# Residual parked in the output rows, twenty tiles for the squares, three sweeps

## The chip, the cores and the metric

One core of one Trainium2 chip runs the whole program. The metric is device time in microseconds; for the kernel before it is the median of three runs. A profiled execution gives the trace.

## What is computed

One layer of a hybrid encoder trunk: 256 tokens, width 2048, hidden width 8192, all in float32. The second half of it, the MLP, is where the change lies:

```python
u = _rms_norm(x, norm_mix_pre[l])
mix = hybrid_mixer(u, ...)                     # three branches, gated, @ w_out
x = x + _rms_norm(mix, norm_mix_post[l])       # the residual, called x1 in the kernel
hdn = jnp.square(jax.nn.relu(_rms_norm(x, norm_mlp_pre[l]) @ w_mlp_up[l]))
x = x + _rms_norm(hdn @ w_mlp_down[l], norm_mlp_post[l])
```

The residual is needed three times: transposed, as the input of the MLP; squared and summed, for the small term that stands for epsilon in the last norm; and at the very end, where the normed MLP output is added to it.

## The kernel before

**Arithmetic.** Every float32 weight is cast to a high part on ScalarE (`whi`, L173) and the rest is kept as a low part by a subtraction on VectorE (`wlo`, L175). A product of two split operands is three TensorE products: high by high, high by low, low by high. All weights come as blocks of 128 x 1024, 512 KB, through SP's queue into a few rotating `raw` buffers (three in L161, six of `raw2` in L1326). `pk` is a pool of 24 tiles of 128 x 512.

**The mixer** ends in `tok` (L208), four column groups of 512 for two token halves. `rstd_of` (L1139) forms a reciprocal root: a sum on VectorE, ScalarE adds the last part, GpSimd raises to -0.5 (L1148). `add_mixed` (L1166) then adds the normed mixer output to `x1`, two tiles of 128 x 2048, in pieces of 512 columns. In this part the order of TensorE, ScalarE, VectorE and GpSimd is the order in which the program is written, up to L1275. TensorE transposes `x1` (`turn`, L1188), `cut` scales and splits it into the sixteen `pk` tiles `upk2`, and the first up products start.

**Up.** For each of 64 hidden blocks of 128, `up(j)` is two halves of 16 matmuls (eight of 512 columns, eight of 256). `hidden(j)` adds two parts of the result, takes the positive part, squares it and keeps it in a `pk` tile, two blocks to a tile.

**Down.** Fourteen sets (`SIZES`) of four hidden blocks go through a scheme of the Strassen and Winograd kind: instead of eight block products, seven (`F[1]` to `F[7]`, six matmuls of 128 x 512 each), at the price of sums. `forms(m)` makes seven combinations of the squares for two hidden blocks, high and low, in two tiles of the tag `fm`; the pool has 16 of them, the room for eight pairs, four sets. Sums of weights are made by `prep` (L1404): one or two additions of 128 x 1024 on VectorE (L1407) and additions by DMA from GpSimd (L1410). The last two sets' worth (eight blocks) goes through a plain `tok` at the end, the tail.

The sets are grouped into sweeps: (3, 4, 4, 3). Within a sweep the seven PSUM sums run over its sets, for one half of the output columns, then for the other. At the end of each such round the seven sums are added into `ys` (`post`, L1446, the operations of L1437): eleven additions on VectorE and one copy on ScalarE; in the first sweep four of the eleven are copies on ScalarE (L1442). Eight rounds make eight of these ends.

**The order of the work.** A list is built (L1520 to L1556) and driven by `drive`. It begins with up halves and six forms, then has 28 slots, one for each set and column half. A slot holds the seven products, three or four up halves (three in the slots named in `THREE`) and those forms for which there is room and whose squares exist. In a slot with four halves products and halves alternate; in one with three, products 4, 7, 1 and 6 follow each other. The additions of a finished round are handed out two with each up half. From L1275 on the scheduler of the framework puts the engines' instructions in order from this list; it may move them where an operand is ready sooner.

**The squares of the residual.** `hidden` for j from 2 to 9 also issues one ScalarE square of 512 columns of `x1` with a running sum (L1357), eight in all, each behind the square of its block; j = 10 and 11 make the two small columns `eps4` on VectorE.

**The end.** In the tail, for each of four column groups and two token halves: add the sum to `ys`, square it, scale by the gain; the gains come as four loads of 256 KB into `pk` tiles, called one by one from `side` at each new weight block. For the last group the reciprocal root is formed and five operations (L1584) add the scaled output to `x1` and five DMAs write the rows.

Of the kernel before, what the change touches and what calls it, by code (L numbers as in the profile page):

```python
# [11 lines left out]
F32 = mybir.dt.float32  # L12
F32R = mybir.dt.float32r
AF = mybir.ActivationFunctionType
ALU = mybir.AluOpType
AX = mybir.AxisListType
# [3 lines left out]
D = 2048  # L20
# [4 lines left out]
EPS = 1e-6  # L25
# [27 lines left out]
def hybrid_block(ctx, tc, xt, x, gains, params, consts, lora, gup, wst, out):  # L53
    nc = tc.nc
    V, A, G, PE = nc.vector, nc.scalar, nc.gpsimd, nc.tensor

    cpool = ctx.enter_context(tc.tile_pool(name="cpool", bufs=1))
# [8 lines left out]
    def nm(s):  # L66
        uid[0] += 1
        return f"{s}_{uid[0]}"
# [7 lines left out]
    def pk():  # L76
        return pkpool.tile([128, 512], F32R, tag="pk", name=nm("pk"), bufs=24)

    def tmp(n=T):
        return tpool.tile([128, T], F32, tag="tmp", name=nm("tmp"), bufs=3)  # L80
# [75 lines left out]
    side = []  # L156
# [125 lines left out]
    def g1(w=T):  # L282
        return rp.tile([128, T], F32, tag="g1", name=nm("g1"), bufs=21)
# [83 lines left out]
    w = {(u, 0): [wpool.tile([128, HALF], F32R, tag=t, name=nm(t), bufs=3) for t in ("whi", "wlo")] for u in range(3)}  # L367
# [662 lines left out]
    for br in ("sb", "fox"):  # L1030
        for s in ("q", "k"):
# [3 lines left out]
            for h in range(4):  # L1035
                ps = unit(upk)
                t = g1()
# [91 lines left out]
    p2 = ctx.enter_context(tc.tile_pool(name="p2", bufs=1))  # L1129
    po = ExitStack()  # L1130
    op = po.enter_context(tc.tile_pool(name="op", bufs=1))

    def gain(n, tiles):

        t = [a if a.dtype == F32 else a.bitcast(F32) for a in tiles]
        return t, [lambda g=g: nc.sync.dma_start(out=t[g], in_=gains[n:n + 1, 512 * g:512 * g + 512]
                                                 .to_broadcast([128, 512])) for g in range(4)]

    def rstd_of(ss, eps, sums):  # L1139

        if sums is None:
            sums = cpool.tile([128, 1], F32, name=nm("ssum"))
            V.tensor_reduce(sums, ss[:, 0:3], AX.X, ALU.add)
            V.tensor_scalar(sums, sums, 1.0 / D, eps, ALU.mult, ALU.add)
            return sums
        r = cpool.tile([128, 1], F32, name=nm("rs"))
        A.activation(r, ss[:, 3:4], AF.Identity, scale=1.0 / D, bias=sums)
        G.tensor_tensor(r, r, cst[:, 2:3], ALU.pow)  # L1148
        return r
# [2 lines left out]
    for f in now:  # L1152
        f()
    loads = []
    x1 = [p2.tile([128, D], F32, tag="x1", name=nm("x1"), bufs=2) for _ in range(2)]
    for c in range(0, D, 512):
        for tt in range(2):
            loads.append(lambda tt=tt, c=c: nc.sync.dma_start(out=x1[tt][:, c:c + 512],
                                                              in_=x[tt * 128:tt * 128 + 128, c:c + 512]))
# [3 lines left out]
    def junk():  # L1163
        return p2.tile([128, 512], F32, tag="junk", name=nm("junk"), bufs=2)

    def add_mixed(tt, c, w):  # L1166
        V.scalar_tensor_tensor(x1[tt][:, c:c + w], mg[tt][:, c:c + w], r2[tt], x1[tt][:, c:c + w], ALU.mult, ALU.add)

# [88 lines left out]
    for b in range(4):  # L1259
        add_mixed(1, 512 * b, 512)  # L1260
        turn(1, b)
# [14 lines left out]
    ss3 = cpool.tile([128, 2, 4], F32, name="ss3")  # L1276
# [11 lines left out]

    SIZES = (3, 4, 4, 3)
    THREE = (18, 20, 21, 23, 24, 25, 26, 27)
    LAST = sum(SIZES)
    AF_ = {1: 0, 2: 1, 4: 2, 7: 3, 5: 4, 6: 5, 3: 6}
    work, posts, sums, hl = [], [], [], {}
# [41 lines left out]
    eps4, sum4 = [], []  # L1337
    ss4 = cpool.tile([128, 2, 4], F32, name="ss4")
    ys = []
    hid, fmh, fml = {}, {}, {}  # L1340

    squares = [(tt, c) for c in range(4) for tt in range(2)]

    def hidden(j, ps):

        b, t = tmp(), tmp()
        A.activation(b, ps[:, T:2 * T], AF.Copy)  # L1347
        V.tensor_tensor(t, ps[:, 0:T], b, ALU.add)
        A.activation(t, t, AF.Relu)
        if j % 2 == 0:  # L1350
            hid[j // 2] = pk().bitcast(F32).rearrange("p (s t) -> p s t", s=4)
        h = hid[j // 2]
        last = A.activation(h[:, 0:4:3] if j % 2 == 0 else h[:, 1:3], t.rearrange("p (s t) -> p s t", s=2), AF.Square)
        if j >= 2 and squares:
            tt, c = squares.pop(0)
            with tc.issue_after(last.ins):
                A.activation(junk(), x1[tt][:, 512 * c:512 * c + 512], AF.Square, accum_out=ss3[:, tt, c:c + 1])  # L1357
        if j in (10, 11):
            e = cpool.tile([128, 2], F32, name=nm("eps4"))
            V.tensor_reduce(e[:, 0:1], ss3[:, j % 2, :], AX.X, ALU.add)  # L1360
            V.tensor_scalar(e[:, 0:1], e[:, 0:1], 1.0 / D, EPS, ALU.mult, ALU.add)
            V.tensor_tensor(e[:, 1:2], e[:, 0:1], e[:, 0:1], ALU.mult)
            V.tensor_scalar(e[:, 1:2], e[:, 1:2], EPS, None, ALU.mult)
            eps4.append(e[:, 1:2])

    def up(j):

        ps = [None]

        def run(hl, half):  # L1370
            if half == 0:
                ps[0] = gps()
            gemm(ps[0], hl[0], hl[1], upk2[8 * half:8 * half + 8], half == 0, half == 1)
            if half:
                posts.append(lambda: hidden(j, ps[0]))

        n = base + 64 * (j // KT) + 2 * (j % KT)
        return [(lambda half=half: wq.pop(0) if wq else parts(wraw(n + half)), lambda hl, half=half: run(hl, half), 2)
                for half in range(2)]
# [15 lines left out]
    def down(q, sb):  # L1395

        d0 = sum(SIZES[:q])
        dn = d0 + SIZES[q] - 1
        Q, R, vx = {}, {}, {}
# [74 lines left out]
    p3 = ctx.enter_context(tc.tile_pool(name="p3", bufs=1))  # L1474

    def fm():
        return p3.tile([128, 7, 128], F32R, tag="fm", name=nm("fm"), bufs=16)

    def split3(m):

        h = hid.pop(m)
        for i in range(2):
            t = fm().rearrange("p a b -> p (a b)")[:, 0:512]
            src = h[:, 0:4:3] if i == 0 else h[:, 1:3]
            hi = t[:, 0:T].rearrange("p (s t) -> p s t", s=2)
            A.activation(hi, src, AF.Copy)
            V.tensor_tensor(t[:, T:].rearrange("p (s t) -> p s t", s=2), src, hi.bitcast(F32), ALU.subtract)
            hp[2 * m + i] = t
# [14 lines left out]
    for j in range(2):  # L1503
        hidden(j, gp[j])
    ups = [it for j in range(2, 64) for it in up(j)]
    made, room = [0], [8]

    def some(n):

        return [ups.pop(0) for _ in range(min(n, len(ups)))]  # L1510

    def form(need=32):

        if room[0] == 0 or 128 - len(ups) < 4 * (made[0] + 1) or made[0] >= need:
            return []
        room[0] -= 1
        made[0] += 1
        return [later(made[0] - 1)]

    work.extend(form())  # L1520
    while made[0] < 2 * SIZES[0]:
        work.extend(some(4) + form())
    drive()
    ys.extend(p2.tile([128, D], F32, tag="y", name=nm("y"), bufs=2) for _ in range(2))
# [3 lines left out]
    NUM = [4] * 28  # L1528
    for g in THREE:
        NUM[g] = 3  # L1530
    assert sum(NUM) == left
    last, count, free = [], 0, 0
    first = [sum(SIZES[:q]) for q in range(len(SIZES) + 1)]

    needs = [2 * (first[q] + d + 1) if sb == 0 else 2 * first[q + 1]
             for q in range(len(SIZES)) for sb in range(2) for d in range(SIZES[q])] + [32] * 3
    for q in range(len(SIZES)):
        for sb in range(2):
            for d, F in enumerate(down(q, sb)):
# [10 lines left out]
                last, count, free = [F[4]], count + 1, sb  # L1550
# [8 lines left out]
    hp = [hp[k] for k in range(4 * LAST, 64)]  # L1559
    g4, loads = gain(1, [pk() for _ in range(4)])  # L1560
    side.extend(loads)

    def spare(n):

        if n < wst.shape[0] - 3:
            return None
        return [p3.tile([128, HALF], F32, tag="raw2", name=nm("kw"), bufs=6).bitcast(F32R) for _ in range(2)]

    home[0] = spare
    for g in range(4):  # L1570
        gs = slice(512 * g, 512 * g + 512)
        for tt, ps in enumerate(tok(hp, 4 if g == 3 else 1)):
            yv = ys[tt][:, gs]
            V.tensor_tensor(yv, yv, ps, ALU.add)
            A.activation(junk(), yv, AF.Square, accum_out=ss4[:, tt, g:g + 1])
            if g == 3:
                r4 = rstd_of(ss4[:, tt, :], None, sum4[tt])
            V.tensor_tensor(yv, yv, g4[g], ALU.mult)
            if g == 2:
                sum4.append(rstd_of(ss4[:, tt, :], eps4[tt], None))  # L1580
            if g == 3:
                for c, w in (0, 512), (512, 512), (1024, 512), (1536, 256), (1792, 256):
                    cs = slice(c, c + w)
                    V.scalar_tensor_tensor(x1[tt][:, cs], ys[tt][:, cs], r4, x1[tt][:, cs], ALU.mult, ALU.add)  # L1584
                    (nc.scalar if c == 512 or w == 256 and c == 1536 else nc.sync).dma_start(
                        out=out[tt * 128:tt * 128 + 128, cs], in_=x1[tt][:, cs])


# [123 lines left out]
```

## Time and profile before

| what | value |
|---|---|
| median of three runs | 1504.24 us (1503.12 to 1506.56) |
| profiled execution | 1505.64 us, of which the span is 1503.8 us |
| granted TensorE clock | 0.998 |
| TensorE busy | 1489.7 us, 8384 matmuls |
| VectorE busy | 1206.8 us |
| ScalarE busy | 938.4 us |
| GpSimd busy | 91.1 us |
| bytes moved by DMA | 312.19 MB, read from HBM 279.24 MB, written 2.10 MB |

The profile's page gives busy times per engine, the span in forty slices, the chain of work that ended last, groups of instructions with their mean duration, and DMA issues with the time to landing. The trace behind it answers for a stretch of time: which instructions ran, what each waited for, and how busy each engine was. In a row of the timeline stand the start, the duration, the engine and line, the operation, the tiles (written <- read) and in brackets the idle time before it and what ended that. PE is TensorE, PEld its weight loads, DVE VectorE, ACT ScalarE, POOL GpSimd, SP the queue that issues most DMAs.

The span falls into the mixer (to about 820 us), the opening of the MLP with up halves alone (to 888 us), the 28 slots (to 1450 us), the tail of plain products (to 1494 us) and the last writes.

### The profile page before, as it was taken

The numbers are of one execution on the slowest core, as the hardware profiler recorded it, in microseconds if no ns is written. First come the engines' busy times: TensorE is split into PE (matmuls) and PEld (weight loads), VectorE is DVE, ScalarE is ACT, GpSimd is POOL, SyncE is SP. The second block draws the span as 40 slices with busy tenths as digits, with TensorE's granted clock in tenths as the row PEclk, the third lists the DMA queues.
The fourth block names the chain that finished last, engine by engine and source line by source line (L and its number), as shares of the span: only waits on it lengthen the run. The fifth ranks groups of instructions, "written<-read, shape, count | busy, mean of one in ns | idle before, by whom it ended". The sixth has DMA issues, their size and how long they took to land.

```text
span 1503.8 us, 22719 instructions
## 1 busy us (share of the span) xinstructions
PE 1489.7 (99%) x8384; PEld 1250.7 (83%) x8384; DVE 1206.8 (80%) x1677; ACT 938.4 (62%) x1435; POOL 91.1 (6%) x151
## 2 busy tenths in 40 slices
PE   9999999999999999999999999999999999999997
PEld 7888888887788887788888888888888888888886
DVE  7965679895688796476657788999899989999996
ACT  7665677545776445564445776776767666767663
POOL 0011003000001000000000000000000000000000
PEclk9999999999999999999999999999999999999999
DMA  8545445454445455345674768879888888889874
GB/s 284 202 150 178 151 158 169 155 182 162 157 167 173 150 192 189 135 165 195 226 243 161 261 179 256 252 223 286 243 269 239 225 279 258 249 259 261 256 216 149
DMA packets 107055, 312.19 MB, mean 208 GB/s; under 512 B 12352, under 2 KB 14400, under 8 KB 106944
## 3 DMA queue, kind: packets, MB, share of 16 engines
q1 hardware_dynamic: 96336, 279.35, 54.8%
q0 software_dynamic: 8064, 29.36, 10.5%
q10 hardware_dynamic: 2544, 2.03, 0.5%
q8 instruction: 66, 1.08, 0.3%
q14 instruction: 45, 0.37, 0.1%
HBM read 279.24 MB, written 2.10 MB: 187 GB/s over the span
## 4 chain that ended last, share of the span: by engine, by line
PE 94%; DVE 2%; ACT 1%; issue 1%; DMA 0%; SPq 0%; POOLq 0%; DVEq 0%; POOL 0%; ACTq 0%
PE gps L235 27%; PE gps L191 22%; PE gps L195 12%; PE gps L220 7%; PE mps L1430 3%; PE mps L1432 3%; PE mps L1431 3%; PE gps L1432 2%; PE gps L1430 2%; PE gps L1431 2%; PE gps L197 2%; DVE wlo L175 1%; PE mps L836 1%; PE gps L359 1%; PE gps L1219 1%
## 5 line engine op out<-in xcount | busy, mean ns | idle before, releaser
L175 DVE TENSOR_TENSOR wlo<-raw,whi 128x1024 fp32r<-128x1024 f32 x570 | 691.3, 1223 | 151.5 <-ACT whi L173 141.8
L173 ACT ACTIVATE whi<-raw 128x1024 fp32r<-128x1024 f32 x570 | 597.9, 1057 | 246.5 <-PE gps L235 71.7
L191 PE MATMUL gps<-pk,whi 128*128 128x512 f32 x1460 | 370.7, 392 | 1.0 <-ACT whi L173 0.8
L191 PEld LDWEIGHTS gps<-pk,whi 128*128 128x128 f32 x1460 | 270.6, 188 | 56.4 <-ACT whi L173 1.7
L235 PE MATMUL gps<-whi,pk 128*128 128x512 f32 x1004 | 253.5, 392 | 0.0
L195 PEld LDWEIGHTS gps<-pk,wlo 128*128 128x128 f32 x1561 | 212.8, 190 | 15.4 <-DVE wlo L175 0.5
L235 PEld LDWEIGHTS gps<-whi,pk 128*128 128x128 f32 x1004 | 186.4, 188 | 40.0 <-issue 1.0
L195 PE MATMUL gps<-pk,wlo 128*128 128x256 f32 x1561 | 218.0, 282 | 0.1
L235 PE MATMUL gps<-wlo,pk 128*128 128x512 f32 x502 | 138.1, 393 | 0.1
L235 PEld LDWEIGHTS gps<-wlo,pk 128*128 128x128 f32 x502 | 93.1, 188 | 20.0 <-DVE wlo L175 0.5
L1347 ACT ACTIVATE tmp<-gps 128x256 f32<-128x256 f32 x64 | 24.6, 385 | 105.2 <-PE gps L197 103.3
L1430 PE MATMUL mps<-whi,fm 128*128 128x512 f32 x224 | 88.6, 396 | 1.4 <-ACT whi L173 1.3
L1431 PE MATMUL mps<-whi,fm 128*128 128x512 f32 x224 | 87.7, 392 | 0.0
L1432 PE MATMUL mps<-wlo,fm 128*128 128x512 f32 x224 | 87.4, 390 | 0.0
L1410 POOL DMA_DIRECT2D raw<-raw x56 | 48.8, 872 | 571.9 <-DVE raw L1407 279.8
L1407 DVE TENSOR_TENSOR raw<-raw,raw 128x1024 f32<-128x1024 f32 x56 | 68.4, 1222 | 0.8
L1430 PE MATMUL gps<-whi,fm 128*128 128x512 f32 x168 | 65.8, 392 | 0.0
L1432 PE MATMUL gps<-wlo,fm 128*128 128x512 f32 x168 | 65.7, 391 | 0.0
L1431 PE MATMUL gps<-whi,fm 128*128 128x512 f32 x168 | 65.5, 390 | 0.0
L220 PE MATMUL gps<-whi,pk 128*128 128x512 f32 x224 | 60.8, 393 | 0.0
L1430 PEld LDWEIGHTS mps<-whi,fm 128*128 128x128 f32 x224 | 42.3, 189 | 9.7 <-ACT whi L173 3.5
L1432 PEld LDWEIGHTS mps<-wlo,fm 128*128 128x128 f32 x224 | 42.1, 188 | 9.4
(358 smaller groups left out, 1743.0 us busy)
## 6 DMA issues: line engine op xcount, KB each, us to landing
raw<-in_wst_dram SPq DMA_DIRECT2D x510, 512.0 KB, 4.3
raw<-raw POOLq DMA_DIRECT2D x56, 512.0 KB, 7.2
x<-in_xt_dram SPq DMA_DIRECT2D x8, 256.0 KB, 5.6
x<-in_x_dram SPq DMA_DIRECT2D x8, 256.0 KB, 5.5
raw<-in_wst_dram SPq DMA_DIRECT2D x6, 256.0 KB, 4.9
pk<-in_wst_dram SPq DMA_DIRECT2D x6, 256.0 KB, 5.1
g<-in_gains_dram SPq DMA_DIRECT2D x4, 256.0 KB, 5.0
pk<-in_gains_dram SPq DMA_DIRECT2D x4, 256.0 KB, 6.8
```

What stands on the lines that cost most here:

```text
L173: A.activation(hi, raw, AF.Copy)
L175: low = lambda: V.tensor_tensor(lo, raw, hi.bitcast(F32), ALU.subtract)
L191: PE.matmul(ps, hi[:, i * 128:i * 128 + 128], pks[i], start=first and i == 0, stop=False)
L195: PE.matmul(ps[:, 0:T], lo[:, i * 128:i * 128 + 128], pks[i][:, 0:T], start=False, stop=False)
L197: PE.matmul(ps, hi[:, (n - 1) * 128:n * 128], pks[n - 1], start=False, stop=True)
L220: PE.matmul(ps[tt], pks[k][:, c:c + 128], w[:, (k - k0) * 512:(k - k0) * 512 + 512], start=k == 0 and part == 0 and w is hl[0], stop=w is ...
L235: PE.matmul(ps[tt], pks[k][:, c:c + 128], w[:, (k - k0) * 512:(k - k0) * 512 + 512], start=k == 0 and part == 0 and w is hl[0], stop=False)
L1407: V.tensor_tensor(R[d, a], R[d, a], R[d, b], ALU.add)
L1410: G.dma_start(out=R[d, a], in_=R[d, b], accum_op=ALU.add)
L1430: PE.matmul(Q[f], a, w, start=d == d0 and i == 0, stop=False)
L1431: PE.matmul(Q[f], b, w, start=False, stop=False)
L1432: PE.matmul(Q[f], a, wl, start=False, stop=d == dn and i == 1)
```

## The change

`x1` moves from the pool that lives to the end (`p2`) to one that is closed before the squares' room is opened (`op`). Each piece that `add_mixed` finishes is written to its place in the output by a DMA on GpSimd's queue, eight of 256 KB. The freed 16 KB of each partition give four more tiles of the tag `fm`: 20, the room for five sets. The sweeps become (5, 5, 4), six rounds instead of eight; `THREE` has twelve slots instead of eight; one more form and four more up halves stand ahead of the first slot. The squares of the residual leave `hidden`. At the end the residual is read back into eight `pk` tiles by SP's queue, two at once and six from `side` behind the gains; a new function `moment` squares it in the second column group of the tail and makes `eps4`; the last additions use these tiles and write from them.

```diff
-    x1 = [p2.tile([128, D], F32, tag="x1", name=nm("x1"), bufs=2) for _ in range(2)]
+    x1 = [op.tile([128, D], F32, tag="x1", name=nm("x1"), bufs=2) for _ in range(2)]
...
         V.scalar_tensor_tensor(x1[tt][:, c:c + w], mg[tt][:, c:c + w], r2[tt], x1[tt][:, c:c + w], ALU.mult, ALU.add)
+        G.dma_start(out=out[128 * tt:128 * tt + 128, c:c + w], in_=x1[tt][:, c:c + w])
...
-    SIZES = (3, 4, 4, 3)
-    THREE = (18, 20, 21, 23, 24, 25, 26, 27)
+    SIZES = (5, 5, 4)
+    THREE = (13, 17, 18, 20, 21, 9, 22, 23, 24, 25, 26, 27)
...
-        last = A.activation(h[:, 0:4:3] if j % 2 == 0 else h[:, 1:3], t.rearrange("p (s t) -> p s t", s=2), AF.Square)
-        if j >= 2 and squares:
-            tt, c = squares.pop(0)
-            with tc.issue_after(last.ins):
-                A.activation(junk(), x1[tt][:, 512 * c:512 * c + 512], AF.Square, accum_out=ss3[:, tt, c:c + 1])
-        if j in (10, 11):
-            e = cpool.tile([128, 2], F32, name=nm("eps4"))
...
+        A.activation(h[:, 0:4:3] if j % 2 == 0 else h[:, 1:3], t.rearrange("p (s t) -> p s t", s=2), AF.Square)
+
+    def moment(tt):
+
+        for c in range(4):
+            A.activation(junk(), x1b[tt, c], AF.Square, accum_out=ss3[:, tt, c:c + 1])
+        e = cpool.tile([128, 2], F32, name=nm("eps4"))
...
-        return p3.tile([128, 7, 128], F32R, tag="fm", name=nm("fm"), bufs=16)
+        return p3.tile([128, 7, 128], F32R, tag="fm", name=nm("fm"), bufs=20)
...
-    made, room = [0], [8]
+    made, room = [0], [10]
...
-    while made[0] < 2 * SIZES[0]:
+    while made[0] < 7:
         work.extend(some(4) + form())
...
+    def back(tt, c):
+        x1b[tt, c] = pk().bitcast(F32)
+        nc.sync.dma_start(out=x1b[tt, c], in_=out[128 * tt:128 * tt + 128, 512 * c:512 * c + 512])
+
+    for tt in range(2):
+        back(tt, 0)
+        side.append(lambda tt=tt: [back(tt, c) for c in range(1, 4)])
...
+            if g == 1:
+                moment(tt)
...
-                    V.scalar_tensor_tensor(x1[tt][:, cs], ys[tt][:, cs], r4, x1[tt][:, cs], ALU.mult, ALU.add)
+                    o = x1b[tt, c // 512][:, c % 512:c % 512 + w]
+                    V.scalar_tensor_tensor(o, ys[tt][:, cs], r4, o, ALU.mult, ALU.add)
                     (nc.scalar if c == 512 or w == 256 and c == 1536 else nc.sync).dma_start(
-                        out=out[tt * 128:tt * 128 + 128, cs], in_=x1[tt][:, cs])
+                        out=out[tt * 128:tt * 128 + 128, cs], in_=o)
```

More of the change, by code (lines that the diff above doesn't have):

```diff
@@ L1340, in hybrid_block @@
     hid, fmh, fml = {}, {}, {}
-    squares = [(tt, c) for c in range(4) for tt in range(2)]
     def hidden(j, ps):
@@ L1352, in hidden @@
         h = hid[j // 2]
-        last = A.activation(h[:, 0:4:3] if j % 2 == 0 else h[:, 1:3], t.rearrange("p (s t) -> p s t", s=2), AF.Square)
-        if j >= 2 and squares:
-            tt, c = squares.pop(0)
-            with tc.issue_after(last.ins):
-                A.activation(junk(), x1[tt][:, 512 * c:512 * c + 512], AF.Square, accum_out=ss3[:, tt, c:c + 1])
-        if j in (10, 11):
-            e = cpool.tile([128, 2], F32, name=nm("eps4"))
[L1360 to L1364, printed above, removed]
+        A.activation(h[:, 0:4:3] if j % 2 == 0 else h[:, 1:3], t.rearrange("p (s t) -> p s t", s=2), AF.Square)
[3 more added lines that the diff above has]
+        e = cpool.tile([128, 2], F32, name=nm("eps4"))
+        V.tensor_reduce(e[:, 0:1], ss3[:, tt, :], AX.X, ALU.add)
+        V.tensor_scalar(e[:, 0:1], e[:, 0:1], 1.0 / D, EPS, ALU.mult, ALU.add)
+        V.tensor_tensor(e[:, 1:2], e[:, 0:1], e[:, 0:1], ALU.mult)
+        V.tensor_scalar(e[:, 1:2], e[:, 1:2], EPS, None, ALU.mult)
+        eps4.append(e[:, 1:2])
     def up(j):
@@ L1561, in hybrid_block @@
     side.extend(loads)
+    x1b = {}
+    def back(tt, c):
[4 more added lines that the diff above has]
+        side.append(lambda tt=tt: [back(tt, c) for c in range(1, 4)])
     def spare(n):
```

## The prediction

> **What bounds the kernel now.** I read the page's busy totals first, then the chain that ended last, then the groups.
>
> ```profile
> PE 1489.7 (99%) x8384; PEld 1250.7 (83%) x8384; DVE 1206.8 (80%) x1677; ACT 938.4 (62%) x1435; POOL 91.1 (6%) x151
> PE 94%; DVE 2%; ACT 1%; issue 1%; DMA 0%; SPq 0%; POOLq 0%; DVEq 0%; POOL 0%; ACTq 0%
> L1437 DVE TENSOR_TENSOR y<-y,mps 128x512 f32<-128x512 f32 x30 | 20.1, 682 | 0.0
> L1437 DVE TENSOR_TENSOR y<-y,junk 128x512 f32<-128x512 f32 x22 | 15.1, 686 | 0.1
> L1437 DVE TENSOR_TENSOR junk<-junk,gps 128x512 f32<-128x512 f32 x16 | 10.9, 681 | 0.0
> L1437 DVE TENSOR_TENSOR y<-y,gps 128x512 f32<-128x512 f32 x12 | 8.2, 680 | 0.0
> ```
>
> TensorE is the bound: 94% of the chain is PE. The change adds and removes no matmul, so it can win only what PE loses by waiting in the stretch where products and up halves are interleaved. Its length follows from PE's timeline and two links of the chain.
>
> ```profile
> 882.72 2.00 PE L191 MATMUL gps<-pk,whi 128*128 128x512 f32 x8
> 885.51 1.78 PE L191 MATMUL gps<-pk,whi 128*128 128x512 f32 x7
> 888.31 0.40 PE L1430 MATMUL gps<-whi,fm 128*128 128x512 f32 x1
> 901.06 1.81 PE gps L191 x8
> 921.76 1.81 PE gps L191 x8
> 1450.37 1.98 PE L235 MATMUL gps<-whi,fm 128*128 128x512 f32 x8
> ```
>
> An up half costs 885.51 - 882.72 = 2.79 us; a slot with four halves recurs after 921.76 - 901.06 = 20.70, so one with three takes 17.91. The 28 slots (20 and 8) need 557.3 us; first product to tail they took 1450.37 - 888.31 = 562.06. **So 4.8 us is the ceiling of the gain there.** The timeline shows where it went: beside 0.1 at 894.6, seven places in which a matmul starts over 0.33 us after the one before, where 0.23 is usual. First and last:
>
> ```profile
> 1196.89 1.06 ACT L173 ACTIVATE whi<-raw 128x1024 fp32r<-128x1024 f32 x1 [3.21 <-DMA raw<-in_wst_dram]
> 1198.69 0.39 PE L1432 MATMUL gps<-wlo,fm 128*128 128x512 f32 x1
> 1199.74 0.50 PE L1430 MATMUL mps<-whi,fm 128*128 128x512 f32 x1 [0.66 <-ACT whi L173]
> 1414.01 0.39 PE L1432 MATMUL gps<-wlo,fm 128*128 128x512 f32 x1
> 1414.44 0.50 PE L1430 MATMUL mps<-whi,fm 128*128 128x512 f32 x1
> ```
>
> Summed over 0.23 a step they lose 1.46 (at 1198.7), 0.83 (1269.1), 0.31 (1319.7), 0.31 (1354.5), 0.89 (1364.9), 0.28 (1401.7), 0.31 (1414.0): 4.4. By slot, counted from 0, that is slots 14-15, 18, 21, 22, 23, 25, 26: all but one in or next to slots with three halves. The busy times in stretches of one slot (us, then PE, PEld, DVE, ACT, POOL, clock, DMA share, GB/s; slots 8, 9, 10, 13, 14, 20, 22, 23, 24, 25) show VectorE nearly as full as PE:
>
> ```profile
> 1054.09:1074.81 20.72, 20.72 (x108) 17.74 (x107) 18.05 (x20) 13.96 (x21) 1.74 (x2) 1.00 0.87 260
> 1074.81:1095.53 20.72, 20.72 (x108) 17.74 (x107) 20.04 (x24) 13.62 (x20) 1.74 (x2) 1.00 0.80 235
> 1095.53:1116.25 20.72, 20.72 (x108) 17.74 (x107) 18.86 (x21) 13.22 (x19) 1.74 (x2) 1.00 0.89 270
> 1157.70:1178.42 20.72, 20.72 (x107) 17.73 (x107) 20.51 (x25) 14.55 (x21) 1.74 (x2) 1.00 0.83 243
> 1178.42:1199.14 20.72, 20.66 (x106) 17.34 (x104) 19.35 (x26) 13.42 (x19) 1.74 (x2) 1.00 0.83 228
> 1299.96:1317.89 17.93, 17.93 (x94) 15.33 (x93) 17.11 (x20) 12.97 (x17) 1.74 (x2) 1.00 0.84 237
> 1335.81:1356.54 20.73, 20.69 (x106) 17.39 (x105) 20.50 (x26) 13.95 (x19) 1.74 (x2) 1.00 0.81 237
> 1356.54:1374.47 17.93, 17.31 (x88) 14.44 (x87) 16.22 (x19) 12.55 (x17) 1.74 (x2) 1.00 0.98 278
> 1374.47:1392.39 17.92, 17.92 (x92) 15.20 (x91) 17.23 (x20) 12.41 (x19) 1.74 (x2) 1.00 0.90 254
> 1392.39:1410.32 17.93, 17.92 (x91) 14.88 (x90) 17.65 (x20) 11.93 (x16) 1.74 (x2) 1.00 0.90 257
> 1268.29 1.28 DVE L1437 TENSOR_TENSOR y<-y,mps 128x512 f32<-128x512 f32 x2
> ```
>
> **The change, part by part: the sweeps.** A round (one sweep, one column half) ends in 11 adds on VectorE, 7 in the first sweep. Eight rounds make 80, which are the four L1437 groups; six make 14 + 44 = 58. Off VectorE go 22 x 0.68 = 15.0 us. An add inside a run costs 0.64 (the pair in 1.28). From slots 9 and 10 (11 adds, no form) a four-half slot needs (20.04 + 18.86 - 7.04) / 2 = 15.9 of VectorE; a form is slot 8 less that, 2.1; slots 24 and 25 (11 adds) give a three-half slot 13.9. By the lists, forms and adds fall so that slots 6, 14 and 22 need over 105% of their PE time (22.7, 23.3, 23.9 of 20.7): they lost 0, 1.46 and 1.20 (slot 22's 0.31 and the 0.89 right behind it), 0.89 in the mean. Of the other three-half slots, 18, 21, 24, 25, 27, with adds, lost 0.83, 0.31, 0, 0.28, 0: mean 0.28; 20 and 26, without, 0 and 0.31: 0.15.
>
> After the change only slot 20 is over 105%: 13.9 + 5 adds + 1 form = 19.2 of 17.9. But three-half slots grow from 8 to 12 (9, 13, 17, 18, 20 to 27), since four more up halves and one form move ahead of the first slot; there VectorE has room, and the 4 x 2.79 us of PE only change place. With adds are 9, 23, 24, 27 (4 x 0.28 = 1.1), without 13, 17, 18, 21, 22, 25, 26 (7 x 0.15 = 1.1), and slot 20 loses 0.9; 0.1 elsewhere. Sum 3.2 against 4.5 (the seven places and 0.1): **-1.3 us**. Bounds: -4.8 if all loss goes; above, every one of the last eight slots loses slot 23's 0.89 (rival B).
>
> **Residual written out.** Eight more POOL issues follow the residual adds, four before the second reciprocal root in POOL's program order, so that one queues behind them, and VectorE's second residual adds, PE's transposes and the MLP's start behind it.
>
> ```profile
> 811.61 2.73 DVE L1167 SCALAR_TENSOR_TENSOR x<-mg,rs,x 128x512 f32<-128x512 f32 x4
> 819.02 0.56 POOL L1148 TENSOR_TENSOR rs<-rs,cst 128x1 f32<-128x1 f32 x1 [8.91 <-ACT rs L1147]
> 821.27 2.73 DVE L1167 SCALAR_TENSOR_TENSOR x<-mg,rs,x 128x512 f32<-128x512 f32 x4
> 835.87 0.53 ACT L1389 ACTIVATE fm<-pk 128x384 fp32r<-128x384 f32 x1
> raw<-raw POOLq DMA_DIRECT2D x56, 512.0 KB, 7.2
> L1410 POOL DMA_DIRECT2D raw<-raw x56 | 48.8, 872 | 571.9 <-DVE raw L1407 279.8 <-DVE wlo L175 235.2 <-DMA raw<-in_wst_dram 47.4
> ```
>
> Four issues at 0.87 from the first add's end (812.3) leave POOL free at about 816, 3 us before 819.02: zero. Were that cover gone, each us late is a us of start. The second four are out by 826 and, at 7.2, landed by 833, before the first form writes room that the residual may have held (835.87). Value 0; bounds 0 to +1 (an issue twice as long: 819.3, and as much again for the landing); a gain is excluded, since nothing on PE's path leaves.
>
> **Squares and read-back.** Eight squares of 0.62, about 0.7 with the read of the sum, leave ScalarE in the first ups, where PE does not wait for it: 0. They and eight 256 KB loads enter the tail, with new waits: a read-back waits on SP for a `pk` tile that the last up halves give back, and the tail's weight loads queue behind it; a square waits on ScalarE for its read-back, with the weight casts behind it, for which VectorE's splits and PE wait. The casts run ahead of PE:
>
> ```profile
> L1357 ACT ACTIVATE junk<-x 128x512 f32<-128x512 f32 x8 | 4.9, 616 | 0.0
> 1456.20 1.06 ACT L173 ACTIVATE whi<-raw 128x1024 fp32r<-128x1024 f32 x1 [2.37 <-DMA raw<-in_wst_dram]
> 1461.25 1.98 PE L235 MATMUL gps<-whi,fm 128*128 128x512 f32 x8
> 1448.00:1452.00 4.00, 4.00 (x23) 3.43 (x22) 4.00 (x7) 2.78 (x5) 0.00 (x0) 1.00 0.42 145
> 1452.00:1456.00 4.00, 4.00 (x19) 3.34 (x18) 4.00 (x6) 1.71 (x3) 0.00 (x0) 1.00 0.60 158
> 1012.64:1033.36 20.72, 20.72 (x107) 17.72 (x106) 19.67 (x24) 14.54 (x21) 1.74 (x2) 1.00 1.01 308
> ```
>
> The cast that ends at 1457.26 is used at 1461.25: a lead of 4.0 us. Six loads that come together (1.57 MB) take 5.1 us at the 308 GB/s of full engines; the engines are idle 3.9 of the 8 us around (0.58 x 4 + 0.40 x 4). 1.2 late, inside the lead. Four squares in a block are 2.8, also inside it. Value 0; bounds 0 to +6.7 (rival C). The final adds read another tile of the same type: 0.
>
> The Trainium skill's page "DMA: Bandwidth & Descriptors", section "Queues, rings and completion order", says that SP has one ring on each of the DMA engines and that each consumes its ring in order. By it a weight load issued behind the six gets none of that idle time for itself and comes 5.1 late, 1.1 beyond the lead, and the sum would be -0.2; no row of the kernel before shows which.
>
> **Sum.** -1.3 + 0 + 0 = -1.3. The profiled execution took 1505.64 (span 1503.8 and 1.8 around it), so 1504.3; it lies 1.4 over the median of the three runs, 1504.24, from which I forecast **1502.9**.
>
> **Rivals.** *A, the losses go.* If they come of VectorE's backlog alone, 15 us less of it removes nearly all: -3.0 to -4.8, 1499.4 to 1501.2. For it: in slots 13 and 22 VectorE is busy 20.5 of 20.7, and PE waits right behind both. Against: slot 23 loses 0.89 with VectorE at 16.22 of 17.93.
>
> *B, three-half slots cost by themselves.* In them four products (4, 7, 1, 6) follow one another without a half between: 24 matmuls at 0.23, 5.5 us of PE, while VectorE has four weight splits and two sums of weights. Eight such slots stand at the end, where five stood. At slot 23's 0.89 each they lose 7.1, the rest 0.8: +3.4, **1507.6, slower**. It decides from 0.83 a slot. For it: slot 23. Against: slots 20, 24 and 27 lost nothing.
>
> *C, the tail.* Read-backs and squares eat the same lead, in order: the six loads' 5.1 and a block of squares 2.8 less 4.0 is 3.9, a second block 6.7. Net +2.6 to +5.4: 1506.8 to 1509.6. It decides where a block of squares stands ahead of a cast that is already over 1.2 us late.
>
> *D, read-backs ahead of a weight load*, without the squares: 5.1 - 4.0 = 1.1 lost, 1504.0. For it: all these loads go through SP's queue. Against: idle engines take most of it. (By the ring rule above it would be so.)
>
> **How the numbers follow.** Forecast (loss of 1.5 to 4.5 in the slots, tail hidden) 0.40; A 0.27; B 0.15; C 0.10; D 0.08. A change under 0.2%, 3.0 us, is about what a measurement of this kernel cannot tell from none. Faster is A, 0.27; same is the forecast, D and a tenth of C, 0.49; slower B and the rest of C, 0.24. Of the chance left out, most lies above 1508; the low end is the ceiling, 1504.24 - 4.8 = 1499.4. The likeliest case's own range is 1501.3 to 1504.2.
>
> **What would show it.** First product to tail 549.6 us (562.06 less four halves, 11.2, and less 1.3); L1437 x58; PE's late starts in slot 20 and the three-half slots; the second POOL root no later behind the last product of the mixer; no PE gap in the tail. Wrong if the slots lose over 7.5 us or under 1.5, or if the tail casts wait on read-back or squares.

## The result, and where the time went

The changed kernel takes 1510.82 us (median of 6 runs, 1509.70 to 1512.27) against 1504.44 for the kernel before (6 runs, 1503.12 to 1506.56). The ratio is 1.0039, with a 95% interval of 1.0028 to 1.0050: slower by 6.4 us, above the forecast and its range. The profiled execution took 1512.27 us, its span is 6.6 us longer than before.

The page of the changed kernel, its span, busy times and DMA issues (KB each, median us from issue to landing):

```profile
span 1510.4 us, 22747 instructions
...
PE 1492.1 (99%) x8384; PEld 1251.8 (83%) x8384; DVE 1196.2 (79%) x1655; ACT 936.6 (62%) x1433; POOL 95.1 (6%) x159
...
out_dram<-x POOLq DMA_DIRECT2D x8, 256.0 KB, 3.8
...
pk<-out_dram SPq DMA_DIRECT2D x8, 256.0 KB, 5.7
```

The groups of instructions of the changed kernel, by line and shape (busy us, mean ns):

```profile
L1436 DVE TENSOR_TENSOR y<-y,mps 128x512 f32<-128x512 f32 x22 | 14.6, 680 | 0.0
L1436 DVE TENSOR_TENSOR y<-y,junk 128x512 f32<-128x512 f32 x16 | 11.0, 685 | 0.0
L1436 DVE TENSOR_TENSOR junk<-junk,gps 128x512 f32<-128x512 f32 x12 | 8.2, 681 | 0.0
...
L1436 DVE TENSOR_TENSOR y<-y,gps 128x512 f32<-128x512 f32 x8 | 5.4, 681 | 0.0
...
L1357 ACT ACTIVATE junk<-pk 128x512 f32<-128x512 f32 x8 | 4.9, 616 | 0.0
```

The change did on VectorE what it says: 22 + 16 + 12 + 8 = 58 adds instead of 80. The four rows lose 15.1 us; VectorE as a whole is 10.6 us less busy, since its total counts time once in which instructions overlap. The end moved the other way. The span divides at PE's marks: the first product, the start of the tail, the last matmul. The timeline of the changed kernel, start and duration in us, with the wait ahead and its releaser in brackets:

```profile
812.29 2.38 POOL L1168 DMA_DIRECT2D out_dram<-x  x4 [2.89 <-DVE x L1167]
...
818.31 0.57 POOL L1148 TENSOR_TENSOR rs<-rs,cst 128x1 f32<-128x1 f32 x1 [3.65 <-ACT rs L1147]
...
898.78 0.40 PE L1429 MATMUL gps<-whi,fm 128*128 128x512 f32 x1
...
1223.51 1.06 ACT L173 ACTIVATE whi<-raw 128x1024 fp32r<-128x1024 f32 x1 [3.48 <-DMA raw<-in_wst_dram]
...
1440.44 0.86 POOL L1409 DMA_DIRECT2D raw<-raw  x1 [8.15 <-DVE wlo L175]
1448.33 2.01 ACT L173 ACTIVATE whi<-raw 128x1024 fp32r<-128x1024 f32 x2 [4.29 <-DMA raw<-raw]
1451.73 0.85 PE L235 MATMUL gps<-whi,fm 128*128 128x512 f32 x3
1471.01 1.06 ACT L173 ACTIVATE whi<-raw 128x1024 fp32r<-128x1024 f32 x1 [1.45 <-PE gps L235]
1473.96 0.63 ACT L1583 ACTIVATE junk<-y 128x512 f32<-128x512 f32 x1 [1.89 <-DVE y L1582]
...
1478.03 1.07 PE L235 MATMUL gps<-wlo,fm 128*128 128x512 f32 x4
1480.11 2.94 ACT L173 ACTIVATE whi<-raw 128x1024 fp32r<-128x1024 f32 x3
1481.20 3.32 PE L235 MATMUL gps<-whi,fm 128*128 128x512 f32 x8 [2.11 <-ACT whi L173]
...
1497.88 2.87 DVE L1595 SCALAR_TENSOR_TENSOR pk<-y,rs,pk 128x512 f32<-128x512 f32 x5 [0.46 <-POOL rs L1148]
1500.67 0.68 DVE L1582 TENSOR_TENSOR y<-y,gps 128x512 f32<-128x512 f32 x1
```

- *Front, -0.7.* The first product starts at 898.78. Before it started at 888.31, and four up halves of 2.79 (11.16) moved ahead of it, which makes 899.47. Two later kernels, E1 and E2, start it at 898.98 and 898.10 with the same work up to there (E2 has two small fills on GpSimd more), so this is taken for the difference of executions. The second root on POOL starts at 818.31, when the four write-outs have long been issued: they hold up nothing here.
- *Slots, +2.05.* From the first product to the tail 552.95 us, where 16 four-half slots of 20.70 and 12 three-half slots of 17.91 make 546.1: 6.8 lost, 4.8 before.
- *Tail, +4.06.* From 1451.73 to the start of the last matmul 47.35 us, 43.29 before. ScalarE's last cast ahead of the squares ends at 1472.07, its next three start at 1480.11. Between stand the two sums of `y` and all eight squares, 6.15 us of work in a row (1473.96 to 1480.11). PE runs out of weights: its last matmul starts at 1478.71, the next at 1481.20.
- *End, +1.22.* Half 1's add at 1500.67 waits behind the five final adds of half 0 (1497.88), though PE was done with half 1 at 1499.5. Before, that add started at 1494.13, within 0.1 us of PE's end.

The sum is -0.69 + 2.05 + 4.06 + 1.22 = 6.6. In the kernel before, ScalarE had a weight cast between the two sums of `y`; below it are that kernel's last matmuls and half 1's add:

```profile
1471.69 0.63 ACT L1575 ACTIVATE junk<-y 128x512 f32<-128x512 f32 x1 [1.93 <-DVE y L1574]
...
1472.33 1.04 ACT L173 ACTIVATE whi<-raw 128x1024 fp32r<-128x1024 f32 x1
1473.28 0.61 ACT L1575 ACTIVATE junk<-y 128x512 f32<-128x512 f32 x1
...
1489.81 4.24 PE L220 MATMUL gps<-kw,fm 128*128 128x512 f32 x18
...
1494.13 0.68 DVE L1574 TENSOR_TENSOR y<-y,gps 128x512 f32<-128x512 f32 x1
```

The changed kernel in stretches of 4 us (us, then busy time and count of PE, PEld, DVE, ACT, POOL, the granted clock, DMA share, GB/s):

```profile
1476.00:1480.00 4.00, 3.10 (x14) 2.24 (x12) 1.22 (x5) 4.00 (x13) 0.00 (x0) 1.00 0.11 46
1480.00:1484.00 4.00, 2.80 (x8) 2.22 (x9) 3.44 (x7) 3.04 (x5) 0.00 (x0) 0.72 0.11 29
1484.00:1488.00 4.00, 4.00 (x17) 3.21 (x16) 1.37 (x2) 1.06 (x1) 0.00 (x0) 0.85 0.83 289
```

ScalarE is full for 4.00 of the first 4 us, PE idles, and so do the DMA engines: SP issues no weight load from 1473.4 to 1482.4, since the tiles for loaded weights come free only behind casts. Then the granted clock falls to 0.5 for 3.41 us: the eight matmuls at 1481.20 take 3.32 where eight take 1.98. So the tail's 4.06 are the gap, 2.27 (2.49 less one start of 0.23), and 1.8 of half clock.

### The profile page after: what moved, and what is told of

Read it like the earlier page. It is cut to its first block, busy times and chain, and to the rows that moved or that the text cites. A ratio compares the mean times of both kernels' runs of the same rounds, so it can differ in the third digit from the quotient of the medians.

```text
span 1510.4 us, 22747 instructions
## 1 busy us (share of the span) xinstructions
PE 1492.1 (99%) x8384; PEld 1251.8 (83%) x8384; DVE 1196.2 (79%) x1655; ACT 936.6 (62%) x1433; POOL 95.1 (6%) x159
## 3 DMA queue, kind: packets, MB, share of 16 engines
q8 instruction: 66, 1.08, 0.3%
## 4 chain that ended last, share of the span: by engine, by line
PE 87%; DVE 5%; DMA 3%; ACT 3%; issue 2%; SPq 0%; ACTq 0%; DVEq 0%; POOLq 0%; POOL 0%
PE gps L235 23%; PE gps L191 22%; PE gps L195 12%; PE gps L220 6%; PE mps L1429 3%; PE mps L1431 3%; PE mps L1430 3%; PE gps L1431 2%; PE gps L1429 2%; PE gps L1430 2%; DMA raw<-in_wst_dram 2%; DVE wlo L175 2%; PE gps L197 1%; ACT whi L173 1%; DMA raw<-raw 1%
```

## The experiments

**Theory.** The eight squares, in two blocks with no weight cast between, use up the casts' lead (the time by which a cast ends ahead of the first matmul that uses it); the gap and the half clock follow, and the late end too. **Rivals**: the read-backs on SP's queue make the weights late; the new sweeps cost time by their three-half slots. Below, "loss" is worked out from PE's matmul starts: the time by which starts come later than the rate at which such matmuls follow one another, added up by slot.

### E1 and E2: the squares spread out, and left out

E1 queues each square behind an earlier weight cast of the tail:

```diff
-            if g == 1:
-                moment(tt)
...
+    def one(tt, c):
+        with tc.issue_after(cast[0].ins):
+            A.activation(junk(), x1b[tt, c], AF.Square, accum_out=ss3[:, tt, c:c + 1])
...
+    for tt in range(2):
+        for c in range(4):
+            hooks.extend([lambda tt=tt, c=c: one(tt, c), *([lambda: None] if c % 2 == 0 else [])])
```

> The changed kernel, but ScalarE's eight squares of the read-back residual no longer stand in two blocks of four ahead of the tail's last weight casts: they are queued one to four at a time behind earlier weight casts of the tail. Theory 1 (the block of squares makes the casts late, PE stands 2.5 us and then runs 3.4 us at half clock): the 4.1 us of the tail come back, the 1.2 us at the end perhaps, so 1505.5 to 1507.8 us against 1510.8; no PE gap over 1 us and no granted clock of 0.5 inside the tail. Rival (the read-backs on the DMA queues make the weights late): 1510 to 1511.5, with the gap in the same place.

E2 takes the squares out:

```diff
+        G.memset(e, 4.0 * EPS)
...
-            if g == 1:
-                moment(tt)
```

> The changed kernel without the eight squares of the residual: the epsilon of the last norm is a constant (the residual's mean square is left out of it, everything else is computed, the residual is written out and read back as before). Theory 1: 1505.5 to 1507 us, the tail at its rate without a gap. Rival, read-backs at fault: no change, 1510 to 1511.5.

E1 takes 1505.81 (11 runs), ratio to the kernel before 1.0009 (1.0000 to 1.0018); E2 1505.26, 1.0005 (0.9996 to 1.0013). E1 lies in the theory's range, E2 0.2 us below it, and neither is near the rival's 1510. The windows of E1 around its squares:

```profile
1470.00:1474.00 4.00, 4.00 (x19) 3.31 (x18) 3.17 (x5) 2.05 (x5) 0.00 (x0) 1.00 0.87 237
1474.00:1478.00 4.00, 4.00 (x19) 3.33 (x18) 2.35 (x7) 4.00 (x12) 0.00 (x0) 1.00 0.56 210
1478.00:1482.00 4.00, 4.00 (x20) 3.30 (x19) 3.93 (x8) 2.44 (x4) 0.00 (x0) 1.00 0.40 131
```

ScalarE is again full for 4 us, and PE does not notice: a sum of `y` and four squares still stand in a row (3.1 us), but casts come before and behind them. The tail takes 43.30 in both, the end is 10.2 us behind the last matmul as before (11.3 in the changed kernel). So about 5.0 of the 6.4 us are where the squares stand, and not that they, or the read-backs, are in the tail.

### E3: the squares moved alone

The kernel before, with `moment` as the change has it, from the residual in SBUF:

```diff
-            tt, c = squares.pop(0)
-            with tc.issue_after(last.ins):
-                A.activation(junk(), x1[tt][:, 512 * c:512 * c + 512], AF.Square, accum_out=ss3[:, tt, c:c + 1])
...
+            if g == 1:
+                moment(tt)
```

> The kernel before (residual stays in SBUF, old four sweeps), with only the eight squares moved from the first up halves into the tail, as the change has them: two blocks of four. Theory 1: +4 to +5.3 us over the kernel before, 1508.5 to 1509.7, with a PE gap of about 2.5 us in the tail and a half clock behind it. Rival, read-backs or the sweeps at fault: within 0.7 us of the kernel before, 1504.4.

1507.92, ratio 1.0026 (1.0015 to 1.0036): +3.3, on the theory's side, but below its range, and the half clock that it expected did not come. Its timeline and windows:

```profile
1478.53 2.11 PE L235 MATMUL gps<-whi,fm 128*128 128x512 f32 x8 [1.21 <-ACT whi L173]
```

```profile
1476.00:1480.00 4.00, 2.79 (x12) 1.99 (x11) 2.11 (x6) 4.00 (x9) 0.00 (x0) 1.00 0.00 0
1480.00:1484.00 4.00, 4.00 (x19) 3.30 (x18) 2.70 (x3) 1.31 (x2) 0.00 (x0) 1.00 0.80 227
```

The gap is there with no read-back in the kernel, but it is 1.60 us, not 2.49, and the clock stays at 1.00. The tail loses 2.1, the end 1.1, as in the changed kernel. That end is also the block's doing: with the block, PE's program has half 1's last products in part ahead of half 0's rest, in E3 as in the changed kernel; in E1 and the kernel before half 0 is finished first. Why the block starts 0.9 later in the changed kernel, counted from the tail's start, stays open.

### E8: two squares more

To lengthen the gap, E8 does the last square of each block of E3 twice.

> The kernel before with the squares in two blocks in the tail (1507.9 us, PE gap 1.6 us, no half clock), and the last square of each block done twice, so that ScalarE's work ahead of the casts is 2 x 0.62 longer. The gap grows to 2.8 us. Theory: from a gap of about 2.5 us on the clock falls to half for 3.4 us (the changed kernel had 2.49 and lost 1.8 more), so 1507.9 + 1.2 + 1.8 = 1510.9 with 0.5 granted behind the gap. Rival (the half clock does not come of the gap): 1509.1, clock at 1.0.

1506.71, faster than E3, and no answer: the planner of the order of work put a weight cast inside each block. Its ScalarE rows:

```profile
1473.28 1.05 ACT L173 ACTIVATE whi<-raw 128x1024 fp32r<-128x1024 f32 x1
...
1477.90 1.04 ACT L173 ACTIVATE whi<-raw 128x1024 fp32r<-128x1024 f32 x1
```

More work, and the gap is gone, because casts come between: E1's result once more, unasked. The tail loses 0.7 there, and the end 1.6, where the order of the last products is changed too.

### E4: the old sweeps with E1's tail

```diff
-    SIZES = (5, 5, 4)
-    THREE = (13, 17, 18, 20, 21, 9, 22, 23, 24, 25, 26, 27)
+    SIZES = (3, 4, 4, 3)
+    THREE = (18, 20, 21, 23, 24, 25, 26, 27)
...
-        return p3.tile([128, 7, 128], F32R, tag="fm", name=nm("fm"), bufs=20)
+        return p3.tile([128, 7, 128], F32R, tag="fm", name=nm("fm"), bufs=16)
...
-    made, room = [0], [10]
+    made, room = [0], [8]
...
-    while made[0] < 7:
+    while made[0] < 2 * SIZES[0]:
```

> The residual written out and read back with the squares spread over the tail as in the first kernel of this set, but the old sweeps: four of 3, 4, 4 and 3 sets, 16 tiles for the squares, eight three-half slots. Theory 1 with the reading that the new sweeps lose 2.0 us more in the slots than the old ones (6.8 against 4.8): 1504.4 to 1505.8, that is 1 to 2.5 us faster than the first kernel of this set. Rival (the sweeps cost nothing, and it is the read-backs landing at the end of the slots that lose the 2.0): the same as the first kernel within 0.7 us.

1506.04, ratio 1.0012 (1.0003 to 1.0020); E1 with the new sweeps 1505.81. That is the rival's answer: the three sweeps with 22 adds fewer are worth 0.2 us, nothing that can be measured. And parking the residual costs what E1 and E4 have over the kernel before, 1.2 and 1.4 us, whatever the sweeps, though the interval of E1 reaches down to 1.0000. Both lose 0.9 to 1.1 in slot 27, where the kernel before lost nothing; that this is the whole of the price isn't shown (see E9).

### E5, E6 and E10: the three-half slots

E5 is E1, and E6 the kernel before, with the second up half one product earlier, so that three products follow one another and not four:

```diff
-work.extend([F[7], F[1], F[6], *some(1), *form(need), F[2], F[5], *some(1), *form(need)])
+work.extend([F[7], F[1], *some(1), F[6], *form(need), F[2], F[5], *some(1), *form(need)])
```

> The first kernel of the set before (changed kernel, squares of the read-back spread over the tail, 1505.8 us), with one thing moved: in a slot of three up halves the second half stands behind product 1 and not behind product 6, so that no more than three products follow one another. Rival B of the prediction (four products in a row with an add or a form in front cost 0.9 each, in slots 9, 20, 23 and 24): those four slots lose under 0.3 each, 2.3 to 3.5 us come back, 1502.3 to 1503.5. Rival (VectorE has too much to do in these slots, whatever their order): the losses stay, 1505.2 to 1506.4.

> The kernel before with the same single move in its eight three-half slots. By rival B slots 18 and 23 (0.82 and 0.88) and the 0.3 of slots 21, 25 and 26 go: 1.7 to 2.6 us, 1502.0 to 1502.9 against 1504.6. By the rival: no change, 1504.1 to 1505.1.

1511.71 (5 runs, ratio 1.0048, 1.0035 to 1.0061) and 1512.43 (1.0045, 1.0031 to 1.0059): both miss everything expected. Slots 9, 20 and 23 of E5 lose 0.11 or less, as rival B would have it, but slot 24 keeps its 0.9, slots 10, 19 and 22 lose 0.96, 0.72 and 1.53 in place of the others (1.3 of the last in product 3 of slot 23, at the bound of the two), and slot 27 loses 6.2. There ScalarE waits for the last accumulate, which took 10.9 us from issue to landing; E6's last took 9.7, where the kernel before has 5.9. From E5:

```profile
1451.37 2.00 ACT L173 ACTIVATE whi<-raw 128x1024 fp32r<-128x1024 f32 x2 [7.34 <-DMA raw<-raw]
```

Which loads beside them slow the accumulates was not tried. Both gaps in PE came with half clock. E5's is 4.70 us long, and PE starts again at 1452.47; the half clock runs from 1450.88, still in the gap, to 1457.71, twice as long as in the changed kernel:

```profile
1450.88:1454.30 3.42, 1.79 (x3) 1.00 (x4) 1.84 (x3) 2.93 (x4) 0.00 (x0) 0.50 0.78 305
1454.32:1457.73 3.41, 3.41 (x9) 2.64 (x8) 3.41 (x5) 1.61 (x4) 0.00 (x0) 0.50 0.37 114
```

E6's is 2.79, PE starts again at 1453.49, and the half clock runs from 1454.89 to 1458.30, as long as in the changed kernel:

```profile
1454.84:1458.25 3.41, 3.41 (x9) 2.64 (x10) 3.41 (x6) 1.61 (x3) 0.00 (x0) 0.51 0.23 55
```

E10 leaves the order and makes slots 12 and 16, in the middle of a round, the three-half ones in place of 9 and 20, where a round's adds fall:

```diff
-    THREE = (13, 17, 18, 20, 21, 9, 22, 23, 24, 25, 26, 27)
+    THREE = (12, 13, 16, 17, 18, 21, 22, 23, 24, 25, 26, 27)
```

> The first kernel of the studies with other three-half slots: 12 and 16, in the middle of a round, in place of 9 and 20, which end and begin one. Theory: a three-half slot loses its 0.7 to 0.95 where a round's adds fall in it (9, 20, 23 and 24), not because products follow one another; then the losses of 9 and 20 go, 1.7 us, 12 and 16 lose under 0.3 each: 1504.0 to 1504.9. Rival (each move only sends the loss to a neighbour, as the reordering did): the sum of the slots' losses stays within 0.6 of 5.3, 1505.3 to 1506.4.

1505.28, ratio 1.0000 (0.9991 to 1.0010), E1 1.0009: just between the two expectations. The losses by slot, in us, from each profiled execution:

| slot | changed | E1 | E9 | E10 | E11 |
|---|---|---|---|---|---|
| 9 (end of a round) | 0.74 | 0.73 | 0.74 | 0 | 0 |
| 20 (start) | 0.95 | 0.94 | 0.94 | 0 | 0.11 |
| 23 (end) | 0.92 | 0.92 | 0.92 | 0.91 | 0.91 |
| 24 (start) | 0.95 | 0.95 | 0.95 | 0.95 | 0.95 |
| 27 (last) | 1.10 | 0.88 | 0 | 0.91 | 0 |
| 7, 8, 11, 16, 22 together | 1.26 | 0 | 1.46 | 2.99 | 0.79 |
| all, with small ones | 6.8 | 5.3 | 6.0 | 6.3 | 3.6 |

Slots 9 and 20 lost because three halves were put there: as four-half slots they lose nothing, and 12 and 16 lose at most 0.1. But the sum over all slots did not fall in E10's execution; E1's 5.3 became 6.3 by the sixth row, which changes from one execution to the next. In slot 16 of the changed kernel and slots 7 and 16 of E9 it is a weight load that lands late (the cast at 1223.51 in the first timeline waits 3.48 for it); in E10's slots 8 and 22 the profile names no load, and this stays open. It is of the size of what E10 gains, so the gain in time is not shown.

### E7, E9 and E12: what the write-out costs in slot 27

In every kernel with slot order kept and the residual written out on POOL's queue, the last accumulate lands late, and PE waits for the weight that it makes. E7 is E1 with the read-backs in pairs behind later weight loads, so that gains are loaded where the kernel before loads them:

```diff
-        nc.sync.dma_start(out=x1b[tt, c], in_=out[128 * tt:128 * tt + 128, 512 * c:512 * c + 512])
+        with tc.issue_after(rawdma[-5].ins):
+            nc.sync.dma_start(out=x1b[tt, c], in_=out[128 * tt:128 * tt + 128, 512 * c:512 * c + 512])
...
-        back(tt, 0)
-        side.append(lambda tt=tt: [back(tt, c) for c in range(1, 4)])
+        for c in 0, 2:
+            side.append(lambda tt=tt, c=c: [back(tt, c), back(tt, c + 1)])
```

> The first kernel of the set before, with the eight read-backs in pairs behind later weight loads on the SP queue, so that the four loads of gains go out where the kernel before has them (two ahead of the last accumulate, two behind it). If the read-backs made the last accumulate late by pushing all four gains beside it (issue to landing 7.6 to 7.8 us in all versions with read-backs, 5.9 in the kernel before), the accumulate takes about 5.9 again, slot 27 loses under 0.2 and the time is 0.9 less: 1504.7 to 1505.1. Rival (the accumulate is late for another reason): slot 27 still loses 0.9, 1505.8. The tail must stay without gaps.

1506.33, ratio 1.0013 (1.0004 to 1.0021). Slot 27 loses 0.91 as before, the accumulate takes 7.6, and the tail has a new gap of 1.0: my theory of the gains falls. E9 is E1 with the write-out on the other queue, E12 the kernel before with the write-out alone:

```diff
-        G.dma_start(out=out[128 * tt:128 * tt + 128, c:c + w], in_=x1[tt][:, c:c + w])
+        nc.sync.dma_start(out=out[128 * tt:128 * tt + 128, c:c + w], in_=x1[tt][:, c:c + w])
```

```diff
         V.scalar_tensor_tensor(x1[tt][:, c:c + w], mg[tt][:, c:c + w], r2[tt], x1[tt][:, c:c + w], ALU.mult, ALU.add)
+        G.dma_start(out=out[128 * tt:128 * tt + 128, c:c + w], in_=x1[tt][:, c:c + w])
```

> The first kernel of the studies (changed kernel, squares spread over the tail, 1505.8 us), with the residual written out by SP's queue and not by POOL's. In every kernel that writes it out on POOL the last accumulate of slot 27 goes out 0.7 us later than in the kernel before, behind the SP weight load and not ahead of it, lands after 7.6 to 7.8 us instead of 5.9, and slot 27 loses 0.9 to 1.1; moving the read-backs behind the gains did not change it. Theory: the eight DMAs that POOL's program has more are the cause; then the accumulate is early again, slot 27 loses under 0.2, 1504.7 to 1505.0. Rival (the read-backs in the tail): slot 27 still loses 0.9, 1505.4 to 1506.2. SP's weight loads behind the write-outs may start the first product later: more than 0.5 us there would be a price of its own.

> The kernel before with one thing added: the eight write-outs of the residual on POOL's queue at the start of the MLP. Nothing is read back, squares and sweeps are the old ones, and the rows are written over at the end. Theory (the eight DMAs that POOL's program has more make its last accumulate go out 1.08 instead of 0.37 us after the third split began, so that the weight load of SP passes it): issue to landing 7.6 to 7.8, slot 27 loses 0.9 to 1.1 where it lost nothing, 1505.4 to 1505.9 against 1504.7. Rival (the read-backs are needed for it): the accumulate at 0.37 and 5.9 us, slot 27 loses nothing, within 0.4 of the kernel before.

The last accumulate by its line, first in the kernel before, then in E12, then in E9 (ns of the issue, start in us; below it us from issue to landing):

```profile
L1410 POOL DMA_DIRECT2D raw<-raw x1: 869/869/869, 1439.5 to 1439.5; - x1
...
DMA to landing us min/median/max: 5.9/5.9/5.9
```

```profile
L1411 POOL DMA_DIRECT2D raw<-raw x1: 864/864/864, 1438.4 to 1438.4; - x1
...
DMA to landing us min/median/max: 7.8/7.8/7.8
```

```profile
L1410 POOL DMA_DIRECT2D raw<-raw x1: 874/874/874, 1440.4 to 1440.4; - x1
...
DMA to landing us min/median/max: 6.0/6.0/6.0
```

In landing and in slot 27 both are as the theory said, and E12 is so in time. E9's time, 1505.84, is not: it lies in the rival's range. Its profiled execution lost 1.46 at weight loads that landed late, where E1's lost nothing; the other executions have no profile. With no read-back in it, E12 loses 1.10 in slot 27; E9, with all read-backs, loses nothing there. The accumulate waits for the same instructions in all of them. Without the eight DMAs on POOL's queue it is issued 0.37 us after the third of VectorE's splits began, with them 1.08 after. SP's next weight load, issued 0.9 us behind it in the kernel before, then follows after 0.2. SP's issue takes 0.33, POOL's 0.86, so the load's issue ends first (4.4 us to landing, 5.9 in the kernel before), and the accumulate takes 7.8. Why POOL's last issue comes later when eight went ahead of it some 620 us earlier isn't shown by any run. E12 takes 1505.70, ratio 1.0004 (0.9995 to 1.0014), E9 1505.84, 1.0003 (0.9993 to 1.0013): the slot can be read in the profile, and the kernel's time hardly tells it. E9, without the loss in slot 27, took no less time than E1.

### E11: the best version

E1 with E9's and E10's edits.

> Both edits together: write-out on SP's queue, and slots 12 and 16 in place of 9 and 20. By both theories 1503.0 to 1504.2, faster than the kernel before (1504.6); by both rivals 1505.3 to 1506.4.

1504.16 us (12 runs, 1502.56 to 1506.06) against 1504.74, ratio 0.9994 (0.9986 to 1.0003), at the upper end of what both theories gave. That is 6.7 us under the changed kernel, and equal to the kernel before within what can be told. Its first product and its tail's start:

```profile
897.91 0.40 PE L1430 MATMUL gps<-whi,fm 128*128 128x512 f32 x1
...
1447.66 0.62 PE L235 MATMUL gps<-whi,fm 128*128 128x512 f32 x2
```

549.75 us, 3.2 less than the changed kernel, and by chance what the prediction gave for it (549.6).

## Why the prediction was wrong, step by step

- *Squares in the tail, value 0: wrong, and the cause.* In place of 0 they cost 4.06 us in the tail and 1.2 at the end. The lead of the casts was right: the gap of 2.27 is the 6.15 of ScalarE's work less 3.9. The price of a block was high enough: four squares take 2.46, I had 2.8, and E1 runs four and a sum without a gap. What failed is that each block was held against the lead for itself. Nothing in the program puts a cast between the two, and the planner put none; two sums of `y` stood in that row as well. Rival C had both blocks in one sum, and a chance of 0.10; its time, 1506.8 to 1509.6, comes nearest. Its condition, a cast already late by read-backs, was not needed (E3).
- *Half clock: in no step.* The rows shown of the kernel before have full clock, and the prediction took a PE gap to cost only its own length. 1.8 us.
- *The order at the end: in no step.* The moved block also changed the order of the last products, 1.2 us (E3 has it without the other edits).
- *Sweeps, -1.3: wrong.* The 58 adds and slot 20's 0.9 were right, the other bounds not. Three-half slots with a round's adds lost 0.74, 0.92 and 0.95 (9, 23, 24), where I took the mean 0.28 of five slots whose losses ran from 0 to 0.83 (slot 23's 0.89, which I put down to slot 22, was not among them); three-half slots without adds lost 0.4 in all, where I took 1.1. Net of slot 27, loss in the slots was 5.7 in the changed kernel and 4.5 in E1, against 4.8 before; E4 with E1 has the sweeps at 0.2. Rival B had the right price, 0.9, for slots that end or begin a round, and the wrong reason: four products in a row run without loss in 12, 13 and 16 (E10), and parting them gains nothing (E5).
- *Residual written out, 0 with bounds 0 to +1: wrong in place.* The cover in front was right (POOL's root at 818.31). A price came 620 us later, 0.9 to 1.1 in slot 27 (E9, E12).
- *Read-back, 0: right.* E2 has all eight loads, no gap in the tail, and 43.30 us for it. On rival D the Trainium skill's page "DMA: Bandwidth & Descriptors", section "Queues, rings and completion order", says that each ring is consumed in order. By it I had a weight load 1.1 us late. No run shows that wait; but the loads went out three, two or one at a time, not six together, so the rule was not put to its test.

## What to carry to other kernels

Work that an engine does in order must be summed over everything that stands between two of its instructions that another engine waits for, not priced by the block. Two blocks that each fit under a lead need not fit together, and an order that puts one of those instructions between them cost the tail nothing here (43.30 us in E1, as without squares in E2). A queue that ran well may be tuned to within a microsecond of another queue's issue, so a few DMAs more on it can cost elsewhere and much later; compare issue and landing of the same transfer in both traces. Work taken off an engine that isn't the bound at the place where PE waits gains nothing (22 adds, 15 us of VectorE: 0.2 us).

## What the runs showed of the hardware

- PE gaps of 2.49 us (changed kernel) and 2.79 (E6) between matmul starts were followed by granted clock 0.5 for 3.41 us, which began 0.6 and 1.4 us after PE had started again. With the gap of 4.70 (E5) it lasted 6.83 us and began 1.6 us before PE started again. Gaps of 1.60 (E3) and 1.02 (E7) brought none. Counted in stretches of 3.41 us from where the clock changes (in E3 and E7 it does so behind the last matmul), PE was busy for 1.30, 0.86 and 0.69 us of the stretch just ahead of the half clock, and for 2.20 and 2.79 of the stretch that holds the gap of E3 and E7. In the order changed, E6, E5, E3, E7:

```profile
1478.35:1481.76 3.41, 1.30 (x6) 0.77 (x5) 1.35 (x6) 3.41 (x9) 0.00 (x0) 1.00 0.00 0
1451.47:1454.88 3.41, 0.86 (x3) 0.43 (x4) 1.41 (x2) 2.50 (x4) 0.00 (x0) 1.00 0.17 65
1447.47:1450.88 3.41, 0.69 (x5) 0.38 (x4) 0.00 (x0) 0.00 (x0) 0.00 (x0) 1.00 1.02 302
1476.33:1479.74 3.41, 2.20 (x10) 1.52 (x9) 1.85 (x6) 3.41 (x7) 0.00 (x0) 1.00 0.00 0
1487.35:1490.76 3.41, 2.79 (x11) 1.52 (x11) 3.40 (x8) 1.64 (x3) 0.00 (x0) 1.00 0.00 0
```

The Trainium skill's page "TensorE: Matmul & The Clock Gate", section "What's actually happening", gives a free-running window of 3413 ns and half clock after an idle one. The length agrees, E5's with two of them. But the gaps of 2.49 and 2.79 us are shorter than the window and were enough, and the section "HAM oscillation — how this bites in real kernels" warns only of gaps above about 3.4: here the measurement decides.

- Of an accumulate on POOL's queue and a weight load on SP's, 512 KB each, both land after 5.9 us if SP's issue begins 0.9 us behind POOL's (kernel before); if it begins 0.2 behind (E12), the load lands after 4.4 and the accumulate after 7.8.
